# A two-layer hybrid encoder: S5 table terms summed in PSUM and on GpSimd, table parameters of layer 1 through DRAM

## Chip, core and metric

The kernel runs on one core of a Trainium2 chip. The metric is the time of one execution on the device in microseconds (us). TensorE (PE) multiplies matrices into PSUM, VectorE (DVE), ScalarE (ACT) and GpSimd (POOL) work on tiles of up to 128 partitions, and SyncE's queue (SP) issues most transfers.

## The reference

Two layers over a sequence of 512 with 1024 channels. Each normalises x, projects it (`h @ w_in`) and splits the result into q, k, v, two inputs of 512 channels and gates. Three mixers run beside each other: attention with 8 heads of two softmaxes each, a Fourier mixer, and a diagonal state-space layer (S5). Their gated sum goes through `w_out`; a gated FFN of 2816 channels with a convolution of width 3 and a gated input embedding follow. All is float32. What the change touches is S5:

```python
def s5_mix(u, a_re, a_im, log_dt, b_re, b_im, c_re, c_im, d):
    ug = u.astype(jnp.float32).reshape(bsz, s_len, SSM_GROUPS, SSM_GROUP_DIM)   # 32 groups of 16
    b_mat = lax.complex(b_re, b_im)
    c_mat = lax.complex(c_re, c_im)
    bu = jnp.einsum('bsgh,gph->bsgp', ug.astype(jnp.complex64), b_mat)
    state = jnp.zeros(bu.shape, jnp.complex64)
    for direction in range(2):
        lam = lax.complex(a_re[direction], a_im[direction])
        dt = jnp.exp(log_dt[direction])[:, None]
        a_bar = jnp.exp(lam * dt)
        b_scale = (a_bar - 1.0) / lam
        a_elems = jnp.broadcast_to(a_bar, (1, s_len, SSM_GROUPS, SSM_STATE))
        _, xs = lax.associative_scan(_ssm_combine, (a_elems, bu * b_scale),
                                     axis=1, reverse=(direction == 1))
        state = state + xs
    y = jnp.einsum('bsgp,ghp->bsgh', state, c_mat).real
    return y + d.reshape(SSM_GROUPS, SSM_GROUP_DIM) * ug
```

## The kernel before

Activations lie with the channels on the partitions, in tiles of 128 x 512. Every float32 product with a weight is made of three matmuls: `unit` loads a weight block (`wr`), ScalarE rounds it to the upper part `wh` and VectorE subtracts for the lower part `wl`; `mm` (L101 to L107) adds wh by hh, wh by hl and wl by hh in PSUM. These are the rows "w<-" of line 106 and most of TensorE's work.

S5 runs over blocks of 8 positions, as matmuls with tables that the kernel makes itself on the chip, once for each layer. It has two parts.

`s5_params` (L281 to L376) makes from the decay rates, for all 32 groups, a table `ptab` of 16 KB on each partition: powers of the decay, scaled input factors, cosines and sines. `cmul` (L241) is a complex product of six operations on the engine that it is given; here most are VectorE's. Layer 1's table stays in SBUF (`self.prm`) in a pool on the right side (`gen0`). Layer 2's is written to DRAM (`par`) during the FFN of layer 1, and read back chunk by chunk (`pt`).

`s5_tables` (L378 to L451) makes the tables of one chunk of four groups; there are eight chunks in each layer. For both directions d: two GpSimd products (L413, L414) give the two terms of v, in buffers tb1 and tb2; VectorE adds them (L415); TensorE multiplies v with `cat` (identity and one more block) in L425; ScalarE takes the result out of PSUM (L426, L427), and it goes to DRAM (tab<-vbt). Then two GpSimd products (L432, L433) give the two terms of an output factor, VectorE adds them (L434), and they go to DRAM. Finally a `cmul` on GpSimd with the products of cosines and sines (co and si, L243 to L248), with tb2 for the second term; GpSimd multiplies si by a column of signs (L449); both go to DRAM. tb1 has two buffers, tb2 one. A Toeplitz block for the near positions (`s5_toeplitz`, L479) ends the tables of a layer: it loads k0 into a tb2 buffer and dd into one of its own, and writes `dtab` to DRAM.

The order on each engine is a scheduler's: the kernel states programs and priorities, the scheduler lays each engine's instructions in one row, and the engine works that row in order. Layer 1's tables are programmed with low priority in the loop over the heads. In it each head projects q and k, rotates them (L537 to L540, the rotary products on GpSimd in rs, with kz the masked copy of k), scores (L578, L579), takes the softmax and multiplies by v (L602). Layer 2's tables are stepped in the FFN of layer 1. Its up half runs over 22 blocks f of 128 channels: gate columns (48 matmuls for gate and value columns together), VectorE takes the gate out of PSUM into one of two buffers gp (L977), the taps of the convolution (ACT L980, DVE L981, L982), gelu (L195 to L198), the value uu (L988), GpSimd's product uu by cv (L989), then its split into ah (ACT L81) and al (DVE L82). Table steps stand at f = 7, 10, 13, 16, 19. The down half goes over 8 blocks of 128 outputs with steps at k = 0, 2, 4, 6. PSUM has 3 buffers "w", 2 "s" and one each of "t", "o", "m"; bursts of L425 use "m" alone in layer 1 and m, o, t, s in layer 2.

## Time and profile before

| | us |
|---|---|
| median of 3 runs (2184.78 to 2190.39) | 2184.79 |
| the profiled execution | 2186.26 |
| its span | 2184.1 |
| TensorE busy | 2101.1 |
| VectorE busy | 1494.1 |
| ScalarE busy | 1015.5 |
| GpSimd busy | 714.1 |

The span goes from the first to the last instruction on the engines; 2.2 us of the execution lie around it. Busy times are sums of durations on an engine. A float32 matmul of the program shows as two records in the trace where its operands are plain float32 (L425: 128 program matmuls, 256 records). "Idle before" a group is the time in which its engine waited just ahead of it, with the instruction whose end released it behind an arrow. The chain of waits follows the work that ended last backwards through what released each step. Layer 1 runs from the start to some 1190 us, layer 2's tables are made in it from 680 to 1110; from then on layer 2 runs with its tables ready.

### The profile page before, as it was taken

The page shows a single profiled execution, that of the slowest core. Times are in us where ns is not written, and L with a number is a line of the kernel's source. Part 1 is how long each engine was busy: PE and PEld are TensorE (multiplying, and loading weights), DVE is VectorE, ACT ScalarE, POOL GpSimd, SP SyncE. Part 2 cuts the span into 40 slices and gives each one's busy share as a digit, 9 for nine tenths or more (in the row PEclk, how much of TensorE's full clock was granted, in tenths as well). Part 3 has the DMA queues.
Part 4 walks back from the last instruction along what each step waited for, and adds up shares of the span by engine and source line. Part 5 has one row for each costly group of instructions (what it writes and reads, how often), then busy time and mean ns, then how long its engine had stood idle before and what let it go on. Part 6 is the DMA issues. An engine that isn't in the chain of part 4 may idle for free.

```text
span 2184.1 us, 28748 instructions
## 1 busy us (share of the span) xinstructions
PE 2101.1 (96%) x10432; PEld 1763.3 (81%) x10432; DVE 1494.1 (68%) x2497; ACT 1015.5 (46%) x1900; POOL 714.1 (33%) x618
## 2 busy tenths in 40 slices
PE   8899889999999999899999999999999999999998
PEld 6778777888888787778878888788888888888886
DVE  7988788566567988875466588764765666665344
ACT  5256656344444443333343577653454444444332
POOL 5488785133003337656512333201320011110000
PEclk9999999999999999999999999999999999999999
DMA  6332233674332244345545311126743323333341
GB/s 200 99 103 93 87 100 116 208 258 152 110 98 89 84 156 130 121 140 153 180 135 162 107 49 59 58 68 215 252 122 97 97 93 97 99 98 90 99 132 57
DMA packets 119327, 265.48 MB, mean 122 GB/s; under 512 B 44401, under 2 KB 50545, under 8 KB 116753
## 3 DMA queue, kind: packets, MB, share of 16 engines
q1 hardware_dynamic: 111408, 252.04, 36.3%
q10 hardware_dynamic: 7776, 11.60, 1.5%
q8 instruction: 82, 1.34, 0.3%
q14 instruction: 61, 0.49, 0.1%
HBM read 221.07 MB, written 44.56 MB: 122 GB/s over the span
## 4 chain that ended last, share of the span: by engine, by line
PE 69%; DVE 8%; POOL 4%; DMA 3%; ACT 2%; issue 2%; ACTq 0%; SPq 0%; POOLq 0%; DVEq 0%
PE w L106 51%; PE s L106 5%; PE w L1140 2%; DVE wl L95 1%; PE s L676 1%; PE o L602 1%; DMA tab<-tb 1%; PE w L1087 1%; PE w L1089 1%; PE w L1088 1%; PE t L702 1%; PE s L578 1%; PE s L579 1%; PE t L699 1%; PE t L700 1%
## 5 line engine op out<-in xcount | busy, mean ns | idle before, releaser
L106 PE MATMUL w<-hh,wh 128*128 128x512 f32 x1536 | 610.2, 398 | 37.3 <-DVE rs L538 10.2
L95 DVE TENSOR_TENSOR wl<-wr,wh 128x512 fp32r<-128x512 f32 x596 | 470.0, 794 | 230.3 <-ACT wh L94 227.3
L106 PE MATMUL w<-hl,wh 128*128 128x512 f32 x1536 | 606.9, 395 | 2.1 <-DVE hl L82 1.9
L106 PE MATMUL w<-hh,wl 128*128 128x512 f32 x1536 | 605.8, 395 | 0.4 <-DVE wl L95 0.4
L94 ACT ACTIVATE wh<-wr 128x512 fp32r<-128x512 f32 x596 | 365.5, 623 | 500.4 <-PE w L106 390.1
L106 PEld LDWEIGHTS w<-hh,wh 128*128 128x128 f32 x1536 | 292.5, 190 | 106.5 <-issue 13.2
L106 PEld LDWEIGHTS w<-hl,wh 128*128 128x128 f32 x1536 | 292.3, 190 | 63.7 <-DVE hl L82 4.9
L106 PEld LDWEIGHTS w<-hh,wl 128*128 128x128 f32 x1536 | 292.2, 190 | 62.4 <-DVE wl L95 1.5
L989 POOL TENSOR_TENSOR uu<-uu,cv 128x512 f32<-128x512 f32 x44 | 70.9, 1612 | 297.8 <-DVE cv L198 297.8
L106 PE MATMUL w<-ah,wh 128*128 128x512 f32 x352 | 138.5, 394 | 3.2 <-ACT ah L81 2.5
L106 PE MATMUL w<-ah,wl 128*128 128x512 f32 x352 | 138.0, 392 | 1.6 <-DVE wl L95 1.6
L106 PE MATMUL w<-al,wh 128*128 128x512 f32 x352 | 137.2, 390 | 0.2 <-DVE al L82 0.2
L186 POOL TENSOR_TENSOR sq<-sq,sq 128x512 f32<-128x512 f32 x18 | 25.3, 1403 | 316.4 <-ACT sq L184 306.3
L585 ACT ACTIVATE pr<-s,mx 128x512 f32<-128x512 f32 x128 | 88.0, 689 | 34.5 <-DVE mx L580 33.8
L580 DVE TENSOR_REDUCE mx<-s 128x1 f32<-128x512 f32 x128 | 85.9, 682 | 26.1 <-PE s L579 25.5
L539 POOL TENSOR_TENSOR rs<-rs,sinr 128x512 f32<-128x512 f32 x32 | 49.1, 1534 | 106.5 <-DVE rs L538 94.9
L106 PEld LDWEIGHTS w<-ah,wl 128*128 128x128 f32 x352 | 66.2, 188 | 17.1 <-DVE wl L95 2.4
L106 PEld LDWEIGHTS w<-ah,wh 128*128 128x128 f32 x352 | 66.1, 188 | 17.1 <-ACT ah L81 2.8
L112 POOL TENSOR_TENSOR rsq<-rmv,mhalf 128x4 f32<-128x4 f32 x22 | 25.7, 1170 | 165.7 <-DVE rmv L145 97.2
L106 PEld LDWEIGHTS w<-al,wh 128*128 128x128 f32 x352 | 66.2, 188 | 14.6 <-DVE al L82 0.5
L592 DVE SCALAR_TENSOR_TENSOR pr<-pr,c,pr 128x512 f32<-128x512 f32 x64 | 59.7, 932 | 1.4
L578 PE MATMUL s<-ks,qs 128*128 128x512 f32 x128 | 54.6, 431 | 5.9 <-ACT pr L585 5.7
(422 smaller groups left out, 4133.1 us busy)
## 6 DMA issues: line engine op xcount, KB each, us to landing
wr<-in_w_in SPq DMA_DIRECT2D x112, 512.0 KB
wr<-in_w_up SPq DMA_DIRECT2D x88, 512.0 KB
tb<-tab SPq DMA_DIRECT2D x16, 1536.0 KB
tab<-tb SPq DMA_DIRECT2D x64, 256.0 KB
wr<-in_w_down SPq DMA_DIRECT2D x32, 512.0 KB
tab<-vbt SPq DMA_DIRECT2D x32, 256.0 KB
wr<-in_w_attn SPq DMA_DIRECT2D x16, 512.0 KB
wr<-in_w_glu SPq DMA_DIRECT2D x16, 512.0 KB
```

The source lines that it names most:

```text
L94: nc.scalar.activation(hi[:, :n], raw[:, c:c + n], AF.Copy)
L95: nc.vector.tensor_tensor(out=lo[:, :n], in0=raw[:, c:c + n], in1=hi[:, :n].bitcast(F32), op=ALU.subtract)
L106: nc.tensor.matmul(ps, lhsT=w[i][a], rhs=b[i], start=start and i == 0 and q == 0, stop=stop and i == n - 1 and q == 2)
L112: self.nc.gpsimd.tensor_tensor(out=y, in0=v, in1=self.mhalf[:, :n], op=ALU.pow)
L186: eng.tensor_tensor(out=sq, in0=sq, in1=acc[c], op=ALU.add)
L539: nc.gpsimd.tensor_tensor(out=rs, in0=rs, in1=sinr, op=ALU.mult)
L578: nc.tensor.matmul(s, lhsT=q[:, c, qs], rhs=kk[:, c], start=True, stop=False)
L580: V.tensor_reduce(mx[:, c:c + 1], s, op=ALU.max, axis=AX.X, negate=True)
L585: nc.scalar.activation(pt, ss[c], AF.Exp, bias=mx[:, c:c + 1], accum_out=(s1, s2)[c][:, qt:qt + 1])
L592: V.scalar_tensor_tensor(out=pr[0], in0=pr[1], scalar=c2, in1=pr[0], op0=ALU.mult, op1=ALU.add)
L989: G.tensor_tensor(out=u, in0=u, in1=c, op=ALU.mult)
L1140: nc.tensor.matmul(ps, lhsT=x[kh * 4 + kt][:, tt * P:(tt + 1) * P], rhs=self.wide(w, kt, wa), start=(kh == 0 and n == 0 and tt % 2 == 0), ...
```

## The change

Five edits. The two terms of v are no longer added on VectorE: each is an operand of its own, and TensorE adds them as two matmuls in one PSUM accumulation, so L425 (now L424) goes from 8 to 16 program matmuls for each chunk, and 32 adds (L415) go from VectorE. tb2 has two buffers. The add of the output terms (L434) stays on VectorE in layer 1 and is GpSimd's in layer 2, 16 adds. The sign of si is no longer multiplied at each chunk (L449, 16 operations on GpSimd); the angle's sine s8 gets it once in a layer, on VectorE, 128 x 64. Layer 1's parameter table lies in the short-lived pool `tmp0`, is written to DRAM and read back by chunk as in layer 2, programmed at a lower priority. Beside these, three constants share one tile, and dd uses a buffer of bc.

```diff
+        V.tensor_scalar(out=s8, in0=s8, scalar1=self.cst[:, 2:3], scalar2=None, op0=ALU.mult)
         f = [c8, s8]
...
-        if self.prm is not None:
-            prm = self.prm[:, ch]
-        else:
-            prm = self.t(pool, "pt", (P, 8, 2 * GC, 8))
-            nc.sync.dma_start(prm, self.par[:, ch])
+        prm = self.t(pool, "pt", (P, 8, 2 * GC, 8))
+        nc.sync.dma_start(prm, self.par[:, ch])
...
         for d in range(2):
-            v = self.t(pool, "tb1", full, bufs=2)
-            t2 = self.t(pool, "tb2", full, bufs=1)
-            G.tensor_tensor(out=v, in0=wsel(2, d, d == 0), in1=bsel(0), op=ALU.mult)
-            G.tensor_tensor(out=t2, in0=wsel(3, d, d == 0), in1=bsel(1), op=ALU.mult)
-            nc.vector.tensor_tensor(out=v, in0=v, in1=t2, op=ALU.add)
-            vb.append(v.rearrange("p g j h -> p g (j h)"))
+            for q in range(2):
+                v = self.t(pool, f"tb{q + 1}", full, bufs=2)
+                G.tensor_tensor(out=v, in0=wsel(2 + q, d, d == 0), in1=bsel(q), op=ALU.mult)
+                vb.append(v.rearrange("p g j h -> p g (j h)"))
...
-                        nc.tensor.matmul(pv[:, q], lhsT=vb[d][:, g + q], rhs=cat[:, g + q], start=True, stop=True)
+                        for z in range(2):
+                            nc.tensor.matmul(pv[:, q], lhsT=vb[d * 2 + z][:, g + q], rhs=cat[:, g + q],
+                                             start=z == 0, stop=z == 1)
...
-            t2 = self.t(pool, "tb2", full, bufs=1)
+            t2 = self.t(pool, "tb2", full, bufs=2)
...
-            nc.vector.tensor_tensor(out=ct, in0=ct, in1=t2, op=ALU.add)
+            (nc.vector, G)[i].tensor_tensor(out=ct, in0=ct, in1=t2, op=ALU.add)
...
-        self.cmul(G, co, si, lo[0], lo[1], hi[0], hi[1], self.t(pool, "tb2", full, bufs=1))
+        self.cmul(G, co, si, lo[0], lo[1], hi[0], hi[1], self.t(pool, "tb2", full, bufs=2))
...
-        G.tensor_scalar(out=si, in0=si, scalar1=self.cst[:, 2:3], scalar2=1.0, op0=ALU.mult, op1=ALU.mult)
...
-        k0 = self.t(pool, "tb2", (P, NG, 16), bufs=1)[0:16]
+        k0 = self.t(pool, "tb2", (P, NG, 16), bufs=2)[0:16]
...
-        dd = self.t(pool, "s5dd", (16, NG + 16))
+        dd = self.t(pool, "bc", (P, 4, GC, 16)).rearrange("p a g h -> p (a g h)")[0:16, :NG + 16]
...
-            self.prm = self.s5_params(i, tq, gp)
+            with tc.high_priority(offset=-LOW // 4):
+                self.par = self.t(self.dp, "par", (P, NCH, 8, 2 * GC, 8), bufs=L)
+                nc.sync.dma_start(self.par, self.s5_params(i, tq, tq))
```

What stands on the engines in a row, at three places. The names are the tiles written and read, with numbers for buffer and use; lines of the code after stand one lower from L413 on, up to two lower further down.

GpSimd in the up half of layer 1's FFN, from one uu product on, before:

```order
L989 TENSOR_TENSOR uu_8547<-uu_8547,cv_8503 128x512
L432 TENSOR_TENSOR tb_1867_8580<-pt_8275,cat_6684 128x512
L433 TENSOR_TENSOR tb_1868_8581<-pt_8275,bc_8273 128x512
L243 TENSOR_TENSOR tb_1869_8586<-pt_8275 128x512
L244 TENSOR_TENSOR tb_1871_8588<-pt_8275 128x512
L395 TENSOR_SCALAR cat_6684<-bc_8598,cst_72 128x4x16
L397 TENSOR_SCALAR bc_8598<-bc_8598 128x64
L245 TENSOR_TENSOR tb_1869_8586<-tb_1869_8586,tb_1871_8588 128x512
L246 TENSOR_TENSOR tb_1870_8587<-pt_8275 128x512
L247 TENSOR_TENSOR tb_1871_8588<-pt_8275 128x512
L248 TENSOR_TENSOR tb_1870_8587<-tb_1870_8587,tb_1871_8588 128x512
L449 TENSOR_SCALAR tb_1870_8587<-tb_1870_8587,cst_72 128x512
```

and after:

```order
L988 TENSOR_TENSOR uu_8613<-uu_8613,cv_8569 128x512
L432 TENSOR_TENSOR tb_1872_8648<-pt_8343,cat_6741 128x512
L433 TENSOR_TENSOR tb_1873_8649<-pt_8343,bc_8341 128x512
L432 TENSOR_TENSOR tb_1874_8654<-pt_8343,cat_6741 128x512
L433 TENSOR_TENSOR tb_1875_8655<-pt_8343,bc_8341 128x512
L434 TENSOR_TENSOR tb_1872_8648<-tb_1872_8648,tb_1873_8649 128x512
L434 TENSOR_TENSOR tb_1874_8654<-tb_1874_8654,tb_1875_8655 128x512
L244 TENSOR_TENSOR tb_1878_8662<-pt_8343 128x512
L394 TENSOR_SCALAR cat_6741<-bc_8671,cst_71 128x4x16
L396 TENSOR_SCALAR bc_8671<-bc_8671 128x64
L243 TENSOR_TENSOR tb_1876_8660<-pt_8343 128x512
L246 TENSOR_TENSOR tb_1877_8661<-pt_8343 128x512
```

The two v products of a chunk stood ahead of the next uu, one output product and the sign with them; now both output products, both terms each, and their adds stand in one row between two uu, and the v products of a chunk stand behind the second one.

VectorE at the end of that row, where al waits for uu, before:

```order
L95 TENSOR_TENSOR wl_8474<-wr_8467,wh_8473 128x512
L95 TENSOR_TENSOR wl_8515<-wr_8512,wh_8514 128x512
L415 TENSOR_TENSOR tb_1804_8279<-tb_1804_8279,tb_1805_8280 128x512
L82 SCALAR_TENSOR_TENSOR al_8377<-uu_8373,ah_8376 128x512
L977 TENSOR_TENSOR gp_1487_6699<-w_8390,rstd_6678 128x512
L95 TENSOR_TENSOR wl_8519<-wr_8512,wh_8518 128x512
L415 TENSOR_TENSOR tb_1806_8284<-tb_1806_8284,tb_1807_8285 128x512
L981 SCALAR_TENSOR_TENSOR cv_8416<-gp_1487_6699,vec_86,cv_8416 128x512
```

and after:

```order
L95 TENSOR_TENSOR wl_8870<-wr_8863,wh_8869 128x512
L95 TENSOR_TENSOR wl_8911<-wr_8908,wh_8910 128x512
L82 SCALAR_TENSOR_TENSOR al_8773<-uu_8769,ah_8772 128x512
L976 TENSOR_TENSOR gp_1493_6755<-w_8786,rstd_6735 128x512
L95 TENSOR_TENSOR wl_8915<-wr_8908,wh_8914 128x512
L980 SCALAR_TENSOR_TENSOR cv_8812<-gp_1493_6755,vec_84,cv_8812 128x512
```

The adds L415 on both sides of al and gp are gone; al still stands ahead of gp.

GpSimd at the start of layer 1's heads, before:

```order
L526 TENSOR_TENSOR wl_1831<-wr_1828,wh_1830 128x512
L842 MEMSET kz_228_1008 64x512
L843 MEMSET kz_228_1008 64x512
L842 MEMSET kz_229_1009 64x512
L843 MEMSET kz_229_1009 64x512
L526 TENSOR_TENSOR wl_1835<-wr_1828,wh_1834 128x512
L432 TENSOR_TENSOR tb_279_1280<-ptab_333,cat_988 128x512
L539 TENSOR_TENSOR rs_1184<-rs_1184,sinr_197 128x512
L539 TENSOR_TENSOR rs_1230<-rs_1230,sinr_197 128x512
```

and after:

```order
L842 MEMSET kz_227_1009 64x512
L843 MEMSET kz_227_1009 64x512
L842 MEMSET kz_228_1010 64x512
L843 MEMSET kz_228_1010 64x512
L524 TENSOR_TENSOR wl_1915<-wr_1908,wh_1914 128x512
L537 TENSOR_TENSOR rs_1185<-rs_1185,sinr_195 128x512
L412 TENSOR_TENSOR tb_269_1249<-pt_1245,bc_1243 128x512
L412 TENSOR_TENSOR tb_270_1251<-pt_1245,bc_1243 128x512
L412 TENSOR_TENSOR tb_271_1253<-pt_1245,bc_1243 128x512
L412 TENSOR_TENSOR tb_272_1255<-pt_1245,bc_1243 128x512
L537 TENSOR_TENSOR rs_1231<-rs_1231,sinr_195 128x512
L538 TENSOR_TENSOR ra_1184<-ra_1184,rs_1185 128x512
```

Before, the rotary products (rs) stood behind kz's memsets and one output product. Now the four v products of the first chunk (pt is what is read back from DRAM) stand between the first rs product and the second.

## Rows read from the trace of the kernel before

**Rows 1.** the page: busy time, share and instructions by engine; chain by engine

```profile
PE 2101.1 (96%) x10432; PEld 1763.3 (81%) x10432; DVE 1494.1 (68%) x2497; ACT 1015.5 (46%) x1900; POOL 714.1 (33%) x618
...
PE 69%; DVE 8%; POOL 4%; DMA 3%; ACT 2%; issue 2%; ACTq 0%; SPq 0%; POOLq 0%; DVEq 0%
```

**Rows 2.** busy us by stage: window, length, PE, PEld, DVE, ACT, POOL, clock, DMA

```profile
120.00:145.00 25.00, 23.53 (x151) 20.68 (x149) 20.43 (x26) 18.52 (x33) 24.90 (x20) 1.00 0.37 112
129.00:359.00 230.00, 205.83 (x1169) 176.72 (x1169) 197.91 (x319) 144.89 (x319) 186.58 (x155) 0.95 0.30 98
785.00:971.00 186.00, 171.96 (x765) 141.02 (x766) 150.81 (x178) 75.93 (x150) 110.74 (x85) 0.97 0.40 126
971.00:1062.00 91.00, 91.00 (x420) 76.05 (x420) 49.18 (x59) 29.14 (x66) 56.81 (x51) 1.00 0.52 160
1062.00:1110.00 48.00, 43.34 (x200) 35.15 (x199) 23.08 (x34) 18.16 (x38) 16.84 (x14) 0.97 0.57 176
```

**Rows 3.** chain of waits in layer 2's up half: start us, us, what

```profile
854.65 1.71 DVE tb L434
856.37 2.98 DMA tab<-tb
859.41 1.55 POOL tb L243
...
873.47 1.27 POOL uu L989
...
876.66 0.69 DVE gp L977
```

**Rows 4.** timeline at the same place: start us, us, instruction, idle before it

```profile
854.12 1.67 POOL L989 TENSOR_TENSOR uu<-uu,cv 128x512 f32<-128x512 f32 x1 [6.44 <-DVE cv L198]
...
873.54 1.73 DVE L415 TENSOR_TENSOR tb<-tb,tb 128x512 f32<-128x512 f32 x1 [2.75 <-POOL tb L414]
```

**Rows 5.** timeline of TensorE, one burst in layer 2

```profile
807.34 0.65 PE L425 MATMUL m<-cat,tb 128*128 128x144 f32 x4
...
809.21 0.50 PE L106 MATMUL w<-hh,wh 128*128 128x512 f32 x1
```

**Rows 6.** groups by line and shape, 0 to 420: busy us, mean ns, idle before

```profile
L425 PE MATMUL m<-cat,tb 128*128 128x144 f32 x128 | 21.7, 293 | 3.7 <-DVE c L590 2.1 <-ACT kfb L427 1.6
...
L415 DVE TENSOR_TENSOR tb<-tb,tb 128x512 f32<-128x512 f32 x16 | 12.2, 766 | 2.8 <-POOL tb L414 2.8
```

**Rows 7.** groups by line and shape, 680 to 1160

```profile
L434 DVE TENSOR_TENSOR tb<-tb,tb 128x512 f32<-128x512 f32 x16 | 18.8, 1176 | 4.7 <-POOL tb L433 4.7
L415 DVE TENSOR_TENSOR tb<-tb,tb 128x512 f32<-128x512 f32 x16 | 18.6, 1161 | 26.3 <-POOL tb L414 26.3
...
L245 POOL TENSOR_TENSOR tb<-tb,tb 128x512 f32<-128x512 f32 x8 | 12.5, 1564 | 0.0
```

**Rows 8.** chain of waits in layer 1's heads

```profile
249.60 6.00 PE w L106 x18
...
259.31 0.60 DVE tb L415
...
285.77 0.68 POOL tb L449
...
391.35 0.66 PE t L595 x4
```

**Rows 9.** chain of waits of the whole span: layer 2's parameters

```profile
765.06 7.23 DMA par<-ptab
772.30 4.87 DMA pt<-par
```

**Rows 10.** timeline of GpSimd at the start of layer 1's heads

```profile
110.80 0.52 POOL L842 MEMSET kz<- 64x512 f32 x1 [1.32 <-DVE ptab L248]
```

**Rows 11.** chain of waits behind the last burst of layer 2

```profile
1080.73 1.95 DMA tb<-kfb
...
1093.97 2.57 PE w L106 x10
```

11 lines of the change are left out of this document (5 added, 6 removed).

## Prediction, made before the change was run

> **What bounds the kernel now.** I read the page first. TensorE is busy 96% of the span, and 69% of the chain that ended last is TensorE work [rows 1]. What lengthens TensorE's queue therefore costs time, except where TensorE already waits for somebody. So the second view is the busy time by stage, for the stages in which the edited code runs [rows 2]. There are three kinds. In layer 1's heads (129 to 359 us), where the tables of layer 1 are made between the heads, TensorE works 205.83 of 230 us, VectorE 197.91 and GpSimd 186.58: everybody is loaded and TensorE idles 24 us. In layer 2's tables during the FFN's up half (785 to 971), TensorE idles 14 of 186 us. In the down half (971 to 1062) it works 91.00 of 91 us at full clock. The third view is the chain of waits, cut to those stages. In the up half it holds hardly any TensorE: it runs from the VectorE add of an output term over the DMA that frees its buffer, through a row of GpSimd table operations, to GpSimd's uu product, on which VectorE's gp (and then TensorE) depends [rows 3].
>
> **TensorE's new matmuls.** Each chunk's burst has 8 program matmuls, each two records in the trace; m, o, t and s take a quarter each. The burst starts at 807.34 and the next matmul at 809.21, so 1.87 us [rows 5]; the change doubles it. Sixteen chunks give +30 us by pace. By the busy row, 21.7 us in layer 1 [rows 6] and as much again taken for layer 2, it would be +43. What of it is exposed depends on the stage.
>
> *Down half of layer 2.* Four bursts fall there or at its edge, and TensorE has no gap: 4 x 1.87 = 7.5, I take **+8**. Low end 6 (the first of the four comes right behind a stall), high end 11 (4 x 2.7, by the busy row: 21.7 over eight chunks).
>
> *Up half of layer 2.* The cycle of one chunk (three FFN blocks) is 40 us: uu at 854.12 [rows 4], a row of GpSimd work until uu at 873.47, then gp at 876.66 [rows 3], for which TensorE waits. Its idle time is 14 of 186 us [rows 2], 3.0 per cycle, and the 1.87 us lie in it. What counts is the chain. Before, between the two uu: uu 1.65, two output products and a wait for the DMA 3.6 (to 859.41), then ten table operations 14.1 [rows 3], in all 19.35. After, by the order: uu 1.65, four output products 5.1 (1.28 each, as the ten and the two come to 1.4 and 1.28 each), two adds, then eight operations (14.1 less L449 and two input products, 3.3 at 1.1, so 10.8). GpSimd adds of 128x512 took 1564 ns here [rows 7], so 3.1 for two. Sum 20.6, with the DMA's wait covered, since 4.4 us of other operations now stand between an add and the reuse of its buffer. That is +1.2 per chunk. Behind uu, the second L415 of the chunk no longer stands between gp and the next taps: -0.6, its length beside no GpSimd work [rows 8]. Three full cycles at +0.6: **+2**. Low end -4: L415 waited 26.3 us for GpSimd in this layer [rows 7], in order, with wl, al and gp queued behind it; where that wait and not uu came last, up to 1.3 us a cycle come back. High end +6, if the two extra us of TensorE come in full.
> The add that moves takes 1176 ns on VectorE and a like one 1564 on GpSimd, a ratio of 1.33 [rows 7]. The Trainium skill, "GPSIMD Engine Reference", section 3.1, gives a two-input add as 1.96 times slower there, which speaks against the move; by it (an estimate) two adds would be 4.6 us and this term +6.5 instead of +2. The trace does not agree with so large a ratio while both engines work.
>
> *Layer 1's heads.* In the chain from 249.6 to 392, 47 TensorE pieces (the first and the last are shown) make 49 of 139 us [rows 8]. So about a third of the 15 us of new matmuls is exposed, +5. VectorE loses 16 adds, 12.2 us [rows 6]; on the chain in that stretch they are four pieces, 2.9 us (the first is in [rows 8]), so 5.5 over the 263 us of the heads (129 to 392). L449 on GpSimd is 0.68 on the chain [rows 8], over the stage -1.3. The sum is **-2**. Low end -10: all 12.2 come back and TensorE's part hides in its 24 us of idle time. High end +8: half of TensorE's part is exposed and VectorE's relief finds another wait behind it. The L434 adds of layer 1 stay on VectorE, no change. The second scratch buffer (tb2) lets the second product of an output term start without waiting for the first add; it is in the low end.
>
> **Layer 1's parameters through DRAM.** The table no longer stays in SBUF; it is written out (2 MB) and read back by chunk. Layer 1 has no such row before, but layer 2 does the same thing: 7.23 us for the write and 4.87 for the first read [rows 9]. The memory in which the table now lies is used next by kz, by qs and by the second rs buffer; before, kz's memset waited only for the last VectorE operation of the parameters, until 110.80 [rows 10]. Now it waits for the DMA's end. VectorE ends the parameters earlier (by the order, five splits moved ahead of them and two adds gone: some -3 us at 0.5 each), so the memory comes free at about 107.5 + 7.2 = 114.7 instead of 110.8. The chunk's read follows, until about 120. On GpSimd, in order behind kz, stand the rotary products of the heads and then four table products that wait for the read; TensorE's first burst now stands ahead of the first score. GpSimd is busy 24.90 of 25 us from 120 to 145 [rows 2], so a late start isn't made up there. On SP the write is queued ahead of the weights of q and k, with loads ahead of need. I take **+4**; low end 0 (other work of GpSimd is put ahead of kz and covers it), high end +8 (the whole 7.23, and the first read).
>
> **The end of layer 2's tables.** The chain runs through the last table products to k0's load into tb2 at 1080.73 and to TensorE at 1093.97 [rows 11]. k0 no longer needs the scratch buffer of the last product, only the one free after the second add: L432, L433, L432, add, L433, L244, add from 1068 make 9.5 (five at 1.28, two at 1.56), so 1077.5 instead of 1080.7. **-3**; ends -5 (TensorE's idle time there, 4.7 of 48 us [rows 2]) and +2 (the extra adds come ahead of the table's last DMA). The load of dd now shares bc's buffer and waits for the last L433 (1074.5); it lands before k0's product is due: nothing, and within the +2 if not. The two new 128x64 scalings on VectorE are shorter than a 128x512 add's 0.60 [rows 8], one stands in front of the start's chain: within its ends. The merged constants cost nothing. L449's going in layer 2 is counted in the row of operations above.
>
> **Sum.** 4 - 2 + 2 + 8 - 3 = +9 on the profiled run's 2186.26 (span 2184.1, 2.2 around it). That run is 1.5 above the median 2184.79 of the three runs, so against the median I predict 2194. The ends add to -13 and +35. About 0.3%, 6.5 us, is what a measurement of this kernel can tell from no change.
>
> **Rivals.**
> *The waits were the price (faster).* L415 sits in VectorE's order ahead of al, gp and wl and waits 26.3 + 2.8 us for GpSimd, and 30.8 us of adds go with it [rows 6, 7]. If these, and not uu, hold TensorE, each term takes its low end: the heads give -10, the up half -4, the tail -5, the start 0, while the down half keeps +6: -13, 2172; with half of it 2178. For it: VectorE is 86% busy in the heads. Against it: when L415 started at 873.54 [rows 4], uu had only just begun, and al needs it, so the wait ended with the thing that was needed anyway. It decides from the point where relief in heads, up half and tail exceeds the 12 us of down half and start.
> *All of TensorE's work is exposed.* +30 by pace, less the tail: about 2212; by the busy row 2225. For it: 69% of the chain. Against it: 14 and 24 us idle in two of the three stages.
> *GpSimd becomes the bound of the up half.* If the two adds and the four products in one row cost 3 more us per chunk than I count (buffers not yet free, port shared with VectorE) and the start costs 8: 4 more for the start and 9 for three cycles, 2207. For it: the chain there is GpSimd's already. The rows of L415 show the two engines in each other's way: 766 ns in layer 1's stretch, 1161 in layer 2's, for the same add [rows 6, 7]. The Trainium skill, "Perfetto Trace Analysis", section "Optimizing Scalar/DVE Operations", says that moving work between these two may not help since they share a read port. By that rule VectorE would get nothing back for the adds moved.
> *It is all hidden.* Down half +6 to +8 against tail and heads: 2183 to 2189, no change.
>
> **How the numbers follow.** The forecast (net +3 to +15) 0.42, of which a quarter lies within 0.3%; faster 0.22; all exposed 0.12; GpSimd 0.10; hidden 0.14. Slower by over 0.3%: 0.31 + 0.12 + 0.09 = 0.52; within 0.27; faster 0.21. The range of 8 in 10 leaves out the far half of the faster case and half of the exposed one: 2174 to 2212.
>
> **What would show it.** Right: the four bursts of the down half at 3.7 us each with TensorE without a gap; uu to uu in the up half near 20.5 and the cycle at 40 to 41; kz's memsets near 115 behind the DMA of the parameters and the first score 3 to 6 us later than before; k0's load at least 2 us nearer to the last burst. Wrong: cycles below 38 us in the up half (VectorE's waits were the cause), heads that end earlier than 391, or a TensorE that fills its idle time in the heads altogether.

## The result: 2204.1 us, slower by 0.8%

The median of three runs is 2204.12 us (2203.86 to 2206.42), against 2184.79 before: a ratio of 1.0083, with a 95% interval of 1.0069 to 1.0097. That is +19.3 us where +9 was predicted. The profiled execution took 2204.12 us, 2202.3 of it span.

Splitting the span at the same events in both traces shows where the 18.2 us of span came from. The first S5 product is the first matmul of layer 1's S5 mixer that uses the finished tables; pg is the gate of layer 1's embedding, eight blocks that VectorE takes out of PSUM behind the FFN; G ends where it begins the last of them.

| stretch of the span | before | after | difference | predicted for its part |
|---|---|---|---|---|
| A: start to the first score of layer 1 | 129.1 | 138.4 | +9.3 | +4 |
| B: to the last score of layer 1 | 249.4 | 243.7 | -5.7 | -2 |
| C: to the first S5 product of layer 1 | 49.6 | 60.5 | +10.9 | no term |
| D: to the first uu of the FFN | 287.5 | 288.8 | +1.3 | none |
| E: to the last of 22 uu, the up half | 248.8 | 244.1 | -4.8 | +2 |
| F: to the last quarter of the last burst | 102.5 | 108.8 | +6.3 | +8 |
| G: to the last pg | 81.8 | 82.3 | +0.5 | -3 |
| H: to the end, layer 2 | 1035.3 | 1035.6 | +0.3 | none |

Layer 1 lost 14.5 us (A to C), and layer 2's tables 3.3 (D to G). F ends where the last quarter of the last burst (the one in PSUM buffer s) starts; that quarter is 0.5 us longer than before and lies in G.

On the page of the kernel after, the busy times by engine and the chain by engine answer to [rows 1]:

```profile
PE 2124.9 (96%) x10688; PEld 1791.9 (81%) x10688; DVE 1465.9 (67%) x2451; ACT 1015.3 (46%) x1900; POOL 714.1 (32%) x618
...
PE 64%; DVE 8%; POOL 6%; issue 3%; ACT 3%; DMA 3%; ACTq 0%; SPq 0%; POOLq 0%; DVEq 0%
```

TensorE's busy time rose by 23.8 us, VectorE's fell by 28.2, and the whole got 18.2 longer: TensorE's own work alone doesn't tell where the time went, since its share of the chain fell from 69% to 64%. The windows that answer to [rows 2], shifted to the same stretches (window, length, then PE, PEld, DVE, ACT, POOL, clock, DMA share, GB/s):

```profile
138.00:368.00 230.00, 215.71 (x1295) 188.50 (x1295) 188.73 (x310) 147.87 (x327) 172.02 (x146) 0.98 0.32 103
801.00:987.00 186.00, 180.78 (x863) 151.10 (x863) 142.64 (x163) 77.95 (x155) 122.47 (x92) 1.00 0.42 129
987.00:1080.00 93.00, 93.00 (x437) 77.79 (x436) 35.64 (x45) 27.66 (x59) 55.32 (x50) 1.00 0.49 152
1080.00:1128.00 48.00, 44.01 (x205) 36.66 (x203) 23.04 (x29) 17.35 (x35) 20.68 (x16) 0.93 0.55 171
```

In the heads TensorE idles 14.3 of 230 us instead of 24, in the up half 5.2 of 186 instead of 14: most of the new matmuls went into idle time there. In the down half it has no gap, as before. At the end of layer 2's tables it idles 4.0 of 48, as before 4.7. The clock there, 0.93 for 0.97, is no difference: in both traces it is at its lower level (0.50 of full, 1.2 GHz) for 6.8 us, from 1105.7 and from 1107.4, and the window of before holds only the start of that.

In the heads the clock does differ. Stage B, the same columns, before and after:

```profile
129.13:378.58 249.45, 225.28 (x1274) 193.42 (x1273) 213.20 (x345) 157.91 (x349) 190.98 (x159) 0.95 0.31 101
138.43:382.16 243.73, 228.62 (x1362) 199.15 (x1361) 197.75 (x326) 155.17 (x342) 177.16 (x150) 0.98 0.32 103
```

TensorE idles 24 us of B before and 15 after, and the granted clock is at its lower level for 24 us of B before and for 8 after. In E it is there for 6.8 us before and not at all after. So where the new matmuls filled idle time, time at the lower level went with it; whether one made the other, no run shows.

**The start of layer 1's heads.** GpSimd's timeline, which answers to [rows 10] (start us, us, engine, line, operation, idle before it with what ended it):

```profile
116.51 0.52 POOL L842 MEMSET kz<- 64x512 f32 x1 [1.20 <-DMA par<-ptab]
...
119.95 1.29 POOL L537 TENSOR_TENSOR rs<-rs,sinr 128x512 f32<-128x512 f32 x1
121.20 4.10 POOL L412 TENSOR_TENSOR tb<-pt,bc 128x512 f32<-128x512 f32 x4
125.27 1.29 POOL L537 TENSOR_TENSOR rs<-rs,sinr 128x512 f32<-128x512 f32 x1
...
130.02 1.05 POOL L433 TENSOR_TENSOR tb<-pt,bc 128x512 f32<-128x512 f32 x1
```

VectorE's timeline beside it:

```profile
116.48 0.01 DVE L536 LOAD_MASK_SELECT rs<-w  x1 [5.01 <-DMA par<-ptab]
...
119.42 12.80 DVE L95 TENSOR_TENSOR wl<-wr,wh 128x512 fp32r<-128x512 f32 x2 [2.18 <-ACT wh L94]
132.15 0.68 DVE L544 SCALAR_TENSOR_TENSOR ra<-ra,qs 128x512 f32<-128x512 f32 x1
```

and TensorE's:

```profile
128.65 0.63 PE L1139 MATMUL w<-wl,hh 128*128 128x256 f32 x4
135.09 2.26 PE L424 MATMUL m<-cat,tb 128*128 128x144 f32 x8 [5.80 <-issue]
...
138.43 1.06 PE L576 MATMUL s<-ks,qs 128*128 128x512 f32 x2
```

kz starts at 116.51, 5.7 us later than before, released by the DMA that writes the parameters out. That much was foreseen in kind. What was not: VectorE needs 12.8 us for two splits wl, one of which takes 12.20 alone; the longest of 596 such splits in the trace of before took 1.81. It ends when GpSimd's unbroken row ends, at 131. Behind it in VectorE's order stands the add that qs needs (L544), behind qs in ScalarE's order the copies of the first burst out of PSUM (L426 at 134.03, L427 at 134.81), and TensorE waits 5.8 us for those until 135.09.

**Behind layer 1's heads.** The chain of waits (start us, us, what) between the last heads and the first S5 product:

```profile
386.89 0.75 PE m L424 x6
...
390.61 3.40 DMA tab<-tb
...
409.42 0.67 ACTq L489
...
412.65 0.73 ACT oh L81
...
413.77 3.79 DMA wr<-in_w_attn
...
419.19 2.55 DMA fraw<-fd
...
433.16 9.67 PE w L106 x34
```

Before, the same stretch of the chain is TensorE from 391.35 on [rows 8] and no wait for tables; now no TensorE piece stands in it from 387.6 to 433.2. (oh is the upper part of the attention's output, fraw what the Fourier mixer loads back from DRAM.) TensorE's own wait is for oh, and the clock falls during it; one row of its timeline, and one of the windows (columns as above):

```profile
428.06 1.65 PE L106 MATMUL w<-oh,wh 128*128 128x512 f32 x3 [4.05 <-ACT oh L81]
```

```profile
426.40:436.60 10.20, 7.65 (x17) 5.59 (x18) 6.68 (x11) 3.95 (x7) 0.39 (x1) 0.50 0.81 310
```

TensorE idles 4.9 us in C (4.05 for oh and 0.9 more), and from 426.4 on, still within the wait, the granted clock is at its lower level (0.50, 1.2 GHz) for 10.2 us; before, C has 0.2 us of idle time and none at the lower level. What that level costs shows in a quarter of a burst: 0.96 us at it (968.63 to 969.59 of before), 0.49 otherwise. So, as an estimate, half of the 7.65 us that TensorE works in that window and the 4.9 us of idle time are 8.7 of the 10.9 us. Three quarters of the last chunk's burst (from 386.73, 391.63 and 397.41), which before all lay ahead of the last score, add 2.9. The last burst of layer 1 starts at 397.41, 19.6 us later than before (377.86).

**The up half of layer 2.** GpSimd's timeline between two uu, which answers to [rows 3, 4]:

```profile
866.53 1.67 POOL L988 TENSOR_TENSOR uu<-uu,cv 128x512 f32<-128x512 f32 x1 [7.27 <-DVE cv L198]
...
872.68 3.00 POOL L434 TENSOR_TENSOR tb<-tb,tb 128x512 f32<-128x512 f32 x2
...
886.37 1.29 POOL L988 TENSOR_TENSOR uu<-uu,cv 128x512 f32<-128x512 f32 x1
```

The row is 19.84 us long without a gap (before 19.35 with a wait for a DMA in it), and the cycle of one chunk fell from 39.9 to 39.3. TensorE waits 3.4 us for gp in 800 to 985, where it waited 8.6 (785 to 971 before). The largest single piece of E lies elsewhere, between the seventh and the eighth uu, where the first chunk of layer 2 begins: 12.28 us instead of 14.91. VectorE's timeline of before shows at that place:

```profile
777.12 0.75 DVE L981 SCALAR_TENSOR_TENSOR cv<-gp,vec,cv 128x512 f32<-128x512 f32 x1 [0.29 <-ACT cv L980]
779.85 1.53 DVE L415 TENSOR_TENSOR tb<-tb,tb 128x512 f32<-128x512 f32 x1 [1.97 <-POOL tb L414]
781.31 0.74 DVE L982 SCALAR_TENSOR_TENSOR cv<-gp,vec,cv 128x512 f32<-128x512 f32 x1
```

The add L415 stood between two taps of one convolution and waited for GpSimd, which had begun only when the parameters landed (777.17); the second tap, gelu and uu stood behind it.

**The end of layer 2's tables.** The last burst in TensorE's timeline, which answers to [rows 5]:

```profile
1081.40 1.14 PE L424 MATMUL m<-cat,tb 128*128 128x144 f32 x8
...
1084.33 1.14 PE L424 MATMUL s<-cat,tb 128*128 128x144 f32 x8
1085.22 0.49 PE L106 MATMUL w<-ah,wh 128*128 128x512 f32 x1
```

and ScalarE's timeline behind it, where k0's load (L481) answers to [rows 11]:

```profile
1091.37 0.54 ACTq L481 DMA_DIRECT2D tb<-kfb  x1
...
1099.46 5.09 ACTq L489 DMA_DIRECT2D dtab<-kfb  x8
1104.60 2.19 ACT L184 ACTIVATE sq<-x 128x512 f32<-128x512 f32 x4 [10.43 <-DMA dtab<-kfb]
1106.69 1.66 ACT L94 ACTIVATE wh<-wr 128x512 fp32r<-128x512 f32 x3
```

A burst takes 3.8 us instead of 1.87 (1081.40 to 1085.22). k0 is loaded 7.0 us behind the start of the last burst's last quarter instead of 13.7, and yet the stretch as a whole is not shorter. Part of the gain went on the way: k0's load takes 2.98 us instead of 1.95, and VectorE's three short operations on it took 1.2 to 1.6 us each instead of 0.68, beside GpSimd's table products, with a split between them; the eight issues of dtab begin 15.1 us behind the start of the last quarter instead of 18.0. Then ScalarE issues the transfers of dtab, makes four squares, and only then the wh for which TensorE waits 4.0 us. Before, ScalarE had nearly the same order, and TensorE waited only 1.1 us for wh, but another 1.7 for a scale of the norm behind it.

### The profile page after: what moved, and what is told of

Read it like the earlier page. It is cut to its first block, busy times and chain, and to the rows that moved or that the text cites. A ratio compares the mean times of both kernels' runs of the same rounds, so it can differ in the third digit from the quotient of the medians.

```text
span 2202.3 us, 29251 instructions
## 1 busy us (share of the span) xinstructions
PE 2124.9 (96%) x10688; PEld 1791.9 (81%) x10688; DVE 1465.9 (67%) x2451; ACT 1015.3 (46%) x1900; POOL 714.1 (32%) x618
## 4 chain that ended last, share of the span: by engine, by line
PE 64%; DVE 8%; POOL 6%; issue 3%; ACT 3%; DMA 3%; ACTq 0%; SPq 0%; POOLq 0%; DVEq 0%
PE w L106 47%; PE s L106 5%; PE w L1139 2%; DVE wl L95 1%; PE s L674 1%; PE o L600 1%; POOL uu L988 1%; DVE cv L980 1%; PE w L1086 1%; PE w L1088 1%; PE w L1087 1%; POOL tb L434 1%; PE s L577 1%; PE s L576 1%; POOL tb L433 1%
## 5 line engine op out<-in xcount | busy, mean ns | idle before, releaser
L95 DVE TENSOR_TENSOR wl<-wr,wh 128x512 fp32r<-128x512 f32 x596 | 484.0, 817 | 286.1 <-ACT wh L94 283.1
L412 POOL TENSOR_TENSOR tb<-pt,bc 128x512 f32<-128x512 f32 x64 | 79.2, 1263 | 16.3 <-DMA pt<-par 16.3
L106 PEld LDWEIGHTS w<-ah,wh 128*128 128x128 f32 x352 | 66.3, 188 | 14.4 <-ACT ah L81 1.5
L112 POOL TENSOR_TENSOR rsq<-rmv,cols 128x4 f32<-128x4 f32 x22 | 24.0, 1092 | 156.8 <-DVE rmv L145 83.2
L524 POOL TENSOR_TENSOR wl<-wr,wh 128x512 fp32r<-128x512 f32 x32 | 45.1, 1411 | 65.8 <-ACT wh L523 59.5
```

What stands on the lines that cost most here:

```text
L95: nc.vector.tensor_tensor(out=lo[:, :n], in0=raw[:, c:c + n], in1=hi[:, :n].bitcast(F32), op=ALU.subtract)
L106: nc.tensor.matmul(ps, lhsT=w[i][a], rhs=b[i], start=start and i == 0 and q == 0, stop=stop and i == n - 1 and q == 2)
L112: self.nc.gpsimd.tensor_tensor(out=y, in0=v, in1=self.mhalf[:, :n], op=ALU.pow)
L412: G.tensor_tensor(out=v, in0=wsel(2 + q, d, d == 0), in1=bsel(q), op=ALU.mult)
L524: nc.gpsimd.tensor_tensor(out=lo, in0=raw[:, c:c + 512], in1=hi.bitcast(F32), op=ALU.subtract)
```

## The experiments

Two questions were open. Which of the five edits costs the time in layer 1, and by which wait? And where did the seven microseconds go that k0 gained? The theory for the start was that the wait of kz for the DMA is one half and the row of table products ahead of the second rotary product the other; its rival was that the DMA is all of it. For the stretch behind the heads the theory was that the doubled matmuls hold back the tables; the rival that VectorE, ScalarE or the DMAs do. Runs sent together share their runs of the kernel before (2184.8 to 2186.4 us), to which the ratios refer. Stage letters are those of the table above.

### One part at a time

**dram_only**: the kernel before with nothing but the parameters of layer 1 through DRAM.

```diff
-            self.prm = self.s5_params(i, tq, gp)
+            with tc.high_priority(offset=-LOW // 4):
+                self.prm = None
+                self.par = self.t(self.dp, "par", (P, NCH, 8, 2 * GC, 8), bufs=L)
+                nc.sync.dma_start(self.par, self.s5_params(i, tq, tq))
```

> The kernel before with one edit: layer 1's parameter table is written to DRAM and read back by chunk; VectorE's adds, single matmuls, the signs and one tb2 buffer stay. Theory A (the start of layer 1's heads waits for the DMA, and the table work behind it is late): the first score 6 to 9 us later than before's 129, 2190 to 2197 us. Rival B (all of the 18 us come from the doubled matmuls): within 3 us of before, 2182 to 2188, whatever the start does.

2196.69 us, 1.0046 (1.0031 to 1.0061). A is 140.2, so +11.1, B 246.7 (-2.7), C 48.8. This edit by itself costs more than half of the whole change, and it costs it in the start. kz begins at 115.23 here, 4.4 us later than before, so the other 6.6 us of A arise behind it.

**dram_psum**: the changed kernel with the output adds back on VectorE and the sign back at each chunk; DRAM path, PSUM addition and two scratch buffers stay.

```diff
-        V.tensor_scalar(out=s8, in0=s8, scalar1=self.cst[:, 2:3], scalar2=None, op0=ALU.mult)
...
-            (nc.vector, G)[i].tensor_tensor(out=ct, in0=ct, in1=t2, op=ALU.add)
+            nc.vector.tensor_tensor(out=ct, in0=ct, in1=t2, op=ALU.add)
...
+        G.tensor_scalar(out=si, in0=si, scalar1=self.cst[:, 2:3], scalar2=1.0, op0=ALU.mult, op1=ALU.mult)
```

> The changed kernel with two edits undone: the output add of layer 2 is on VectorE again, and the sign is multiplied at each chunk on GpSimd. What is left is the DRAM table and the two matmuls in PSUM with two tb2 buffers. Theory A: the start and the late end of layer 1's tables stay, the up half of layer 2's tables loses 0 to 5 us of what it gained: 2203 to 2210. Rival (the moved output adds are what gained in the up half, by more): 2210 to 2215. If those two edits cost: under 2203.

2198.2 us, 1.0058 (1.0039 to 1.0077): some 6 under the change, though the two intervals touch, so the two edits that were undone seem to cost time together (vector_out and sign_per_chunk, below, take them one by one), and 1.5 above dram_only, no difference that these runs can tell. The stages do differ: B -8.5, C +8.8, E -3.5, F +6.5, G -6.9 against dram_only. Adding in PSUM and the second scratch buffer, which this comparison doesn't separate, shorten the heads and pay it back behind them; in layer 2 they gain in the up half and at the end and pay in the down half. (H is 5.6 longer in this profile; see the last section.)

**add_only**: the kernel before with layer 2's output adds on GpSimd.

```diff
-            nc.vector.tensor_tensor(out=ct, in0=ct, in1=t2, op=ALU.add)
+            (nc.vector, G)[i].tensor_tensor(out=ct, in0=ct, in1=t2, op=ALU.add)
```

> The kernel before with one edit: layer 2's output add on GpSimd. Theory A (the up half's chain runs through GpSimd's row between two uu; the add there costs 1.2 a chunk but the DMA wait and VectorE's add go): 2181 to 2187. Rival (GpSimd is the bound and the adds come on top): 2188 to 2194.

2182.38 us, 0.9979 (0.9970 to 0.9989): moving these adds to the slower engine is a small gain by itself.

### Layer 1

**l1_vector_add**: the changed kernel with layer 1's v added on VectorE again, and so the single matmuls in layer 1.

```diff
+            if i == 0:
+                v = self.t(pool, "tb1", full, bufs=2)
+                t2 = self.t(pool, "tb2", full, bufs=2)
+                G.tensor_tensor(out=v, in0=wsel(2, d, d == 0), in1=bsel(0), op=ALU.mult)
+                G.tensor_tensor(out=t2, in0=wsel(3, d, d == 0), in1=bsel(1), op=ALU.mult)
+                nc.vector.tensor_tensor(out=v, in0=v, in1=t2, op=ALU.add)
...
+                        if i == 0:
+                            nc.tensor.matmul(pv[:, q], lhsT=vb[d][:, g + q], rhs=cat[:, g + q], start=True, stop=True)
```

> The changed kernel with layer 1's input terms added on VectorE again and one matmul each; layer 2 as changed. Theory A1 (the stall of some 11 us behind layer 1's heads comes from the doubled matmuls, which make the last chunk's table late on the one bank m): the stall goes, the start stays late by 9: 2191 to 2197. Rival A2 (the table's end is late because the parameters came late): the stall stays, 2200 to 2206.

2209.98 us, 1.0108 (1.0091 to 1.0125): slower still, above both theories. A 142.7, B 250.4 (+6.7 against after), C 54.6 (-5.9). Without 15 us of TensorE's work the heads take longer: TensorE idles 28 us of B instead of 15, and 17 us of B lie at the clock's lower level instead of 8. Behind the heads the wait for oh is gone, but TensorE still idles 4.5 us in 410 to 430 for others (2.8 for GpSimd's scale of the norm, 1.4 for ath), and the chain still goes over dtab and the loads of fraw. So the doubled matmuls are not the whole reason for the wait behind the heads, and undoing them in layer 1 is no cure.

**chunk0_vector**: the changed kernel with the four v products of layer 1's first chunk on VectorE, which takes them out of GpSimd's row at the start.

```diff
-                G.tensor_tensor(out=v, in0=wsel(2 + q, d, d == 0), in1=bsel(q), op=ALU.mult)
+                (nc.vector if i == 0 and ch == 0 else G).tensor_tensor(out=v, in0=wsel(2 + q, d, d == 0), in1=bsel(q), op=ALU.mult)
```

> The changed kernel, but the four input products of layer 1's first chunk run on VectorE, so that no table product stands between the rotary products on GpSimd. Theory A (of the 9.3 us by which the first score is late, 5.7 are kz's wait for the DMA, the rest are the four products and the VectorE operation that is held up for 12 us beside GpSimd's unbroken run): the first score at 133 to 136, no wl over 3 us near it. Rival (the DMA and its read alone make the start): 137 to 139, as changed. Total 2198 to 2204 if the rest of layer 1 follows, 2204 to 2208 if the table's end decides.

2195.09 us, 1.0041 (1.0026 to 1.0056). GpSimd's and VectorE's timelines at that place:

```profile
116.79 0.52 POOL L842 MEMSET kz<- 64x512 f32 x1 [1.29 <-DMA par<-ptab]
...
120.23 2.51 POOL L537 TENSOR_TENSOR rs<-rs,sinr 128x512 f32<-128x512 f32 x2
122.71 2.48 POOL L538 TENSOR_TENSOR ra<-ra,rs 128x512 f32<-128x512 f32 x2
132.20 1.29 POOL L537 TENSOR_TENSOR rs<-rs,sinr 128x512 f32<-128x512 f32 x1 [7.01 <-DVE rs L536]
```

```profile
119.58 7.96 DVE L412 TENSOR_TENSOR tb<-pt,bc 128x512 f32<-128x512 f32 x4 [2.07 <-DMA pt<-par]
127.47 1.28 DVE L95 TENSOR_TENSOR wl<-wr,wh 128x512 fp32r<-128x512 f32 x2
```

kz waits for the DMA as in after (116.79), but GpSimd's row ends at 125.2, no split is held up (0.68 each; what waits beside that row now are VectorE's four products, 7.96 us), and the first score comes at 134.96, 5.8 us later than in the kernel before where after has 9.3. What is left is the 6.0 us by which kz is late. So of after's 9.3 us in A, some 6 are the DMA and 3.5 the row of GpSimd operations. The shares are not the same in every order of the row: dram_only and sign_per_chunk have kz only 4.4 us late and the first score 11.0 to 11.1. B is 5.8 shorter than after as well; TensorE idles 10.6 us of it instead of 15.1, and 3.4 us lie at the clock's lower level instead of 8. The scheduler's order of the heads changed with the edit, and which of its moves did that was not tried.

**sign_per_chunk**: the changed kernel with the sign of si at each chunk again (L449 of before).

```diff
-        V.tensor_scalar(out=s8, in0=s8, scalar1=self.cst[:, 2:3], scalar2=None, op0=ALU.mult)
...
+        G.tensor_scalar(out=si, in0=si, scalar1=self.cst[:, 2:3], scalar2=1.0, op0=ALU.mult, op1=ALU.mult)
```

> The changed kernel with one edit undone: the sign is multiplied at each chunk on GpSimd. Theory A (the edit itself saves 16 short operations, but it changes the scheduler's order of layer 1, and with it the table's end comes later): the first S5 product of layer 1 some 7 us earlier than the changed kernel's 442.7, 2195 to 2200. Rival (layer 1's late end has nothing to do with the sign): 2204 to 2210.

2196.66 us, 1.0049 (1.0032 to 1.0066): 7.5 us faster than after, with 16 operations more on GpSimd. A is 140.1 (+1.7), B 239.1 (-4.6), C 56.9 (-3.6), D 285.7 (-3.1). In its trace GpSimd makes both rotary products (117.40 and 119.89) ahead of the four table products (123.64), where after has them on both sides. That doesn't help the start: a split on VectorE is held up there too (9.27 us), and the first score comes later than in after. That points to the row beside VectorE, and not, as the theory for the start had it, to the products standing ahead of the second rotary product. The gain lies behind: TensorE idles 10.8 us of B instead of 15.1, and 3.4 us of B lie at the clock's lower level instead of 8. The scaling that takes 16 operations away is one VectorE operation in the parameters of each layer, and the scheduler lays the rows another way behind it. That the order and not the operations cost the 7.5 us is what fits; only the sum is measured.

**dtab_from_sp**: the changed kernel with the transfers of dtab issued by SP instead of ScalarE.

```diff
-            nc.scalar.dma_start(dtab[j * 16:P, j], kfb[0:P - j * 16, 1])
+            nc.sync.dma_start(dtab[j * 16:P, j], kfb[0:P - j * 16, 1])
...
-                nc.scalar.dma_start(dtab[0:j * 16, j], kfb[(7 - j) * 16:112, 0])
+                nc.sync.dma_start(dtab[0:j * 16, j], kfb[(7 - j) * 16:112, 0])
```

> The changed kernel with one edit: the 15 transfers of the Toeplitz block (dtab) are issued from SP's queue and not from ScalarE's, in both layers. Theory A (behind layer 1's heads ScalarE is held by the table's late end and then by issuing these transfers for 4 us, before oh, whose memory the first load of the Fourier part waits for; TensorE waits for those loads): from the last burst of layer 1 to the first S5 product 41 to 43 us instead of 45.3, total 2200 to 2203. Rival (the loads of the Fourier part are late for another reason, or SP's queue holds them up now): 45 or more, 2204 to 2212.

2195.82 us, 1.0039 (1.0027 to 1.0052), over six runs from 2191.13 to 2198.37, of which the profiled one is the lowest: the median is 8.3 us under after, the profile's span 13.0, so the stages below show more than a usual run gained. In ScalarE's timeline of after the eight issues stand ahead of the gates of S5 (idle in brackets counts the time without computing):

```profile
405.71 4.38 ACTq L489 DMA_DIRECT2D dtab<-kfb  x8
410.14 0.63 ACT L625 ACTIVATE ga<-ga 128x512 f32<-128x512 f32 x1 [6.43 <-DMA dtab<-kfb]
```

In the chain of waits of dtab_from_sp, ScalarE's gates and the weight load are gone:

```profile
407.02 3.83 DMA dtab<-kfb
...
410.96 3.02 DMA fraw<-fd
...
425.26 7.39 PE w L106 x31
```

From the last burst to the first S5 product it takes 37.0 us instead of 45.3 (50.4 before, but there TensorE works without a wait). Here the fraw loads start at 410.96 instead of 419.19. ScalarE's issuing was in the chain: without it TensorE's wait for oh is gone, the clock stays at its upper level through C, and C is 8.5 us shorter in this profile; what is left (52.0 for 49.6) is about the size of the three quarter bursts. G is 4.3 shorter too, and TensorE's wait for wh is not in its list of waits. The Trainium skill, "DMA: Bandwidth & Descriptors", section "Issuing engines are not separate DMA queues", says that issuing on several engines only saves the sequencer's time, which is usually small against the transfer. The trace agrees for one issue (0.32 to 0.67 us in the chain of after, against 3.83 us for the transfer in the chain of dtab_from_sp), but not for eight in a row: 4.38 us on ScalarE, ahead of work for which others wait.

### The end of layer 2's tables

**vector_out**: the changed kernel with layer 2's output adds on VectorE.

```diff
-            (nc.vector, G)[i].tensor_tensor(out=ct, in0=ct, in1=t2, op=ALU.add)
+            nc.vector.tensor_tensor(out=ct, in0=ct, in1=t2, op=ALU.add)
```

> The changed kernel with one edit undone: layer 2's output add is on VectorE again. Layer 1's order is the same. Theory A (in the tail behind the last burst the adds on GpSimd stand in k0's chain and eat the gain of the second scratch buffer; in the up half they gained): the stretch from the last burst to the last pg 5 to 6 us shorter than the changed kernel's 82.3, the up half 2 to 3 longer than its 244.1: 2198 to 2203. Rival (the tail's missing gain has another cause): no change in the tail, 2204 to 2208.

2203.34 us, 1.0079 (1.0064 to 1.0094): no difference from after in the sum. G is 76.2 instead of 82.3. Its ScalarE timeline:

```profile
1099.34 5.71 ACTq L489 DMA_DIRECT2D dtab<-kfb  x8
1105.09 1.68 ACT L94 ACTIVATE wh<-wr 128x512 fp32r<-128x512 f32 x3 [8.00 <-DMA dtab<-kfb]
1106.67 2.18 ACT L184 ACTIVATE sq<-x 128x512 f32<-128x512 f32 x4
```

Here the wh stand ahead of the four squares, and TensorE's wait for them (4.0 us in after) is not in its list of waits; nor is the clock at its lower level in G, where after has 6.8 us of it. So part of the time that k0 gained was given back behind dtab, by ScalarE's order. This run doesn't prove the order alone: dtab's issues also begin 12.1 us behind the start of the last quarter, for 15.1 in after, since VectorE's operations on k0 take 0.68 us each. E is 243.0, not longer than after's 244.1: next to PSUM addition the moved adds bring the up half nothing. Against the gain in G stand A +1.2, B +1.7, D +1.3 and H +4.9.

### Layer 1 left alone

**up_half_only**: the kernel before with only layer 2 changed: two scratch buffers there, PSUM addition and the output adds on GpSimd for its first four chunks, which fall in the up half; the down half keeps its single matmuls.

```diff
+        two = i == 1 and ch in (0, 1, 2, 3)
...
-            t2 = self.t(pool, "tb2", full, bufs=1)
+            t2 = self.t(pool, "tb2", full, bufs=1 + i)
...
-            nc.vector.tensor_tensor(out=ct, in0=ct, in1=t2, op=ALU.add)
+            (G if i == 1 and ch in (0, 1, 2, 3) else nc.vector).tensor_tensor(out=ct, in0=ct, in1=t2, op=ALU.add)
```

> The kernel before, layer 1 untouched, with the changed parts only where TensorE had idle time: in layer 2 two scratch buffers, and for its first four chunks (the up half) two matmuls in PSUM and the output add on GpSimd; the last four chunks with VectorE's adds and single matmuls. Theory A (the up half gains 3 to 5, the down half loses nothing, the tail gains 3 to 5 from the second scratch buffer): 2175 to 2181. Rival (the gain of the up half is given back later): 2183 to 2188.

2180.76 us, 0.9978 (0.9969 to 0.9987), G 76.6 and E 248.0. The stretch from the seventh to the eighth uu is 12.26, but at the end of the up half, where the later chunks begin with L415 again, the last two blocks take 34.2 us instead of 30.5. What lengthens them is not shown: with L415 in every chunk (before, no_psum) they take 30.5 and 30.2.

**up_half_sign**: the same with layer 2's sign in the angle.

```diff
+        if i == 1:
+            V.tensor_scalar(out=s8, in0=s8, scalar1=self.cst[:, 2:3], scalar2=None, op0=ALU.mult)
...
+        if i == 0:
+            G.tensor_scalar(out=si, in0=si, scalar1=self.cst[:, 2:3], scalar2=1.0, op0=ALU.mult, op1=ALU.mult)
```

> The kernel of up_half_only with the sign put into the angle in layer 2 only. Theory A (GpSimd's row between two uu is the up half's chain, one operation of 1.0 to 1.5 us goes from it in each chunk): 2 to 5 us under up_half_only's 2180.8, 2176 to 2179. Rival (the chain has another wait there): 2180 to 2182.

2180.49 us, 0.9969 (0.9958 to 0.9980), E 245.8, with 33.6 us for the last two blocks. The total lies where the rival had it, no gain that these runs can tell. A version that keeps the PSUM addition for the chunk behind the last two blocks too was not tried.

**no_psum**: up_half_sign without the PSUM addition, so only buffers, sign and output adds.

```diff
-        two = i == 1 and ch in (0, 1, 2, 3)
+        two = False
```

> The kernel of up_half_sign without any doubled matmul: all input terms are added on VectorE, single matmuls; two scratch buffers, output adds of the first four chunks on GpSimd and the sign in the angle in layer 2. Theory A (taking VectorE's input add out of the up half, where it stands ahead of al and gp, is worth 1 to 3 us more than the doubled matmuls cost there): 1 to 3 us over up_half_sign. Rival (the gain comes from the scratch buffer, the moved add and the sign alone): the same or up to 3 us under it.

2180.31 us, 0.9971 (0.9957 to 0.9984). E is 247.7, 1.9 more than with PSUM addition, and the total is the same, so in this form TensorE's adding brings nothing in the sum: from the seventh to the eighth uu it is 3.6 us shorter, in the last two blocks 3.4 longer. It is L415 that goes with the first of these: 14.4 to 15.1 us in all five profiles with L415 in layer 2's first chunk (before, dram_only, add_only, no_psum, no_psum_dtab_sp), 11.4 to 12.4 in the nine without.

**no_psum_dtab_sp**: no_psum with layer 2's dtab issued by SP.

```diff
+        q = nc.sync if i == 1 else nc.scalar
...
-            nc.scalar.dma_start(dtab[j * 16:P, j], kfb[0:P - j * 16, 1])
+            q.dma_start(dtab[j * 16:P, j], kfb[0:P - j * 16, 1])
```

> The kernel of no_psum, with layer 2's 15 dtab transfers issued from SP's queue instead of ScalarE's. Theory A (behind the last burst ScalarE stands behind these transfers, and wh, which TensorE needs, stands behind ScalarE): from the last burst to the last pg 2 to 4 us under no_psum's 76.9, 2176 to 2179. Rival (the transfers hold up the weights of the next stage in SP's queue instead): 2180 to 2184.

2183.63 us, 0.9990 (0.9981 to 1.0000): not better than no_psum. G is 75.1 instead of 76.9, but H in its profile is 5.0 longer, at a place that the edit doesn't touch.

no_psum and up_half_sign are 0.3% faster than the kernel before and 1.1% faster than the change. The changed kernel with layer 1's table back in SBUF and all else as changed was not tried.

## Why the prediction was right in sign and range, and too low

**The down half** (+8, ends 6 and 11): right. TensorE has no gap (93.00 of 93), and the bursts take 3.8 to 3.9 us as worked out by the pace. The four of them make +6.3 in F and 0.5 in G, so 6.8: the first of the four took 2.95 us before, right behind a stall and with the clock at its lower level (0.50 from 967.4 to 970.8), and not 1.87; the low end of 6 had allowed for that stall.

**The start** (+4, ends 0 and +8): the mechanism was right, the term mis-sized; +9.3 lies outside its ends. Two things were missing. The write of the parameters takes 9.2 us, from its issue to the issue of the read that waits for it, where 7.23 was taken from [rows 9]. SP's queue of after shows what stands ahead of it:

```profile
106.49 0.33 SPq L518 DMA_DIRECT2D wr<-in_w_in  x1
107.28 0.33 SPq L826 DMA_DIRECT2D par<-ptab  x1
...
116.45 0.33 SPq L391 DMA_DIRECT2D pt<-par  x1
```

A weight load of 512 KB is issued 0.8 us ahead of the write, whose own packets move from 109.67 to 115.88, 6.2 us, about as long as in layer 2 before (765.88 to 771.91); it is the start that comes later. In dram_only, with the load ahead of it issued 5.1 us earlier, the same write takes 7.6 us. The prediction had looked at SP's queue for what the write holds up, and not for what holds up the write. And the order of GpSimd at that place was known, with the four products between two rotary products, but the prediction put them behind both, and put no price on what such a row does to VectorE. The trace of before had the hint: at 115.34 one add L434 took 4.26 us on VectorE beside an unbroken GpSimd row, and ended at 119.60, in that row's first gap (119.05 to 119.67). chunk0_vector shows this part to be 3.5 us.

**Layer 1's heads** (-2, ends -10 and +8): B is -5.7, inside the ends. l1_vector_add, which undoes PSUM addition in layer 1 alone, has B at 250.4, so that edit, with the order that goes with it, is what shortens the heads. TensorE's part was hidden in idle time, which fell from 24 to 15 us of B. The prediction had no term for the clock, which is at its lower level 16 us less; how the 5.7 us divide between that and VectorE's relief is not shown.

**The table's end of layer 1**: the step that was left out, +10.9, more than any other term. The prediction ended the stage at 392, with the last matmuls of the heads, and asked only what the heads lose. But the tables have a due time of their own, the first S5 product, and before they met it without a wait. With the last burst 19.6 us later that slack was gone, and the chain went over k0, dtab and the loads of fraw. In GpSimd's groups of the span's first 440 us, the wait of the output products for the burst grew (line, shape; busy us, mean ns; idle before and what ended it):

```profile
L432 POOL TENSOR_TENSOR tb<-pt,cat 128x512 f32<-128x512 f32 x16 | 18.0, 1123 | 36.7 <-PE m L424 30.5 <-DMA tab<-tb 6.1
```

against 17.0 us behind the burst (L425) in the first 420 us of before. All four scratch buffers are operands of the burst now, and no output product can start ahead of its end. How much of the 19.6 is this, the late start and the reads by chunk, the runs don't separate: in l1_vector_add, with single matmuls, TensorE still waits. That ScalarE's issuing of dtab is the larger part of the 10.9 us is shown by dtab_from_sp: 8.5 us in a profile that is faster than its median by 4.7. The stage's time is idle time (4.9 us), the 10.2 us at the clock's lower level that begin in it, and three quarter bursts.

**The up half** (+2, ends -4 and +6): -4.8, wrong in sign. Two steps failed. The first is the cycle: +0.6 was predicted, -0.6 is the mean of the three full cycles, -1.8 in all. The GpSimd row was put at 20.6 us and is 19.84 (the adds took 1.5 each in it where 1.56 was taken, the four output products 4.5 together instead of 5.1), longer than before's 19.35, and the cycle is shorter all the same: TensorE's wait for gp fell by 5.2 us, and the clock, 6.8 us of E at its lower level before, stays at the upper one. So the row between two uu was not what set the cycle alone; the argument against the rival of the waits, that al needs uu anyway, was read at one place and taken for all. The second is the place where layer 2's first chunk begins, -2.6: the prediction counted three full cycles and left the edges out, and there L415 waited for products that waited for a DMA, with a tap of the convolution behind it. The profiles above, and no_psum against up_half_sign as an edit by itself, show that this piece goes with L415. The rest of the cycle's gain goes with no one edit: the mean cycle is 39.6 us in sign_per_chunk and in no_psum, 39.3 in vector_out and 39.7 in add_only. The larger price for two adds on GpSimd, 4.6 us, that the prediction estimated from the Trainium skill ("GPSIMD Engine Reference", section 3.1) was not paid: they took 3.00. On its other rule from the Trainium skill ("Perfetto Trace Analysis", section "Optimizing Scalar/DVE Operations"), by which the moved adds would bring VectorE nothing, the totals come out both ways: add_only is 0.2% faster than before, vector_out the same as after.

**The end of layer 2's tables** (-3, ends -5 and +2): the step was right and its effect was not. k0 came nearer by 6.7 us, more than the 2 that were asked for, and G is +0.5. 3.9 of the 6.7 us were lost again between k0's load and dtab. For the rest nobody had asked what stands behind dtab on ScalarE: four squares ahead of the wh, 4.0 us of TensorE's time. vector_out, with the other order, has G at 76.2, and dtab_from_sp, with dtab off ScalarE, at 78.0.

That the sum came out within the range is in part luck. It lies outside the net +3 to +15 that the prediction gave most weight, and the errors partly cancel: +5.3 at the start, +10.9 and +3.5 for the two ends of tables, against -3.7 in the heads, -6.8 in the up half, -1.7 in F, and +1.6 in D and H, for which there was no term.

## What to carry to other kernels

Work that runs in the background of a stage has an end with a date of its own; ask by how much it meets that date before the change, and what its end has to go through, as well as what it costs the stage. Price an order on GpSimd by what it does to VectorE too, and look in the trace of before for a VectorE operation of several times its usual length beside a row like it. DMA issues on a computing engine stand in that engine's order: what lies behind them waits for every one. Look at the granted clock of a stage, before and after, beside its idle time: here the two moved together.
